# Two heads' low-part score passes on 64 rows each, side by side, in an fp32r attention stage

## Chip, cores and metric

The kernel runs on one core of a Trainium2 chip. The metric is the device time of one execution in microseconds; the kernel before is given as the median of three runs. Engines are named as the profile names them: PE (TensorE, with its weight loads as PEld), DVE (VectorE), ACT (ScalarE), POOL (GpSimd), SP (SyncE, which issues most transfers).

## What is computed

Two transformer blocks follow each other; the change touches the attention of the first. It has two kinds of heads over 1024 tokens and 256 context tokens, with a head size of 64:

```python
s_loc = einsum(q_block, k_window) * scale      # "a": 8 query heads on 2 key heads, a band of 128
s_ctx = einsum(q_block, k_ctx) * scale         # both kinds also see the context
p = softmax(concat([s_loc + mask, s_ctx, sink]))
o = p_loc @ v_window + p_ctx @ v_ctx
...
s_loc = einsum(q_block, k_rows) * scale + rpb  # "b": 8 heads, a neighbourhood in a 16 x 64 grid
```

The rest of the program (projections, two gated feed-forwards, a gated linear attention) is left as it is.

## The kernel before

fp32 products are made of fp32r passes: an operand is split into a high and a low part, and the products of the parts are summed in PSUM.

The attention is a list of 64 units x: 32 of kind "a" (8 token blocks, 4 pairs of heads), then 32 of kind "b" (4 pairs of heads, 8 token blocks). A unit is 128 queries of two heads, e = 0 and 1. An inner block has three key tiles of 128 and two of context, 640 score columns; the first and last token block have two key tiles, 512 columns. Units 0 to 3, 28 to 32, 39, 40, 47, 48, 55, 56 and 63 are the narrow ones.

Keys of a head stand stacked on 128 rows: `stack_k` (line 867) turns key tiles with PE and writes the high part to one half of the rows and the low part to the other. Queries stand doubled on both halves, once with their high parts and once with their low parts (`conv_q`, line 888, for two units at a time). So one pass over the 128 rows with the high query gives high x high and high x low, and a second one with the low query gives low x high and low x low.

A unit goes through these steps, each a function:

- `f_s(x, e)`, lines 936 to 950: the scores of one head, two passes (high, then low query), each over the local and the context columns in their own PSUM bank. A score tile takes two banks, and there are two of them (`ps_s`, bufs=2), which the heads use in turn.
- `f_max(x, e)`, line 961: DVE adds mask or bias and takes the row's extreme, in one operation that reads the scores; it frees the score tile.
- `f_exp(x, e)`, line 971: ACT.
- `f_pt(x, g)`, lines 981 to 998: PE turns up to four tiles of 128 x 128 of the probabilities into a tile `pp` (bufs=3). For g = 0 ACT copies it out (line 993) and POOL makes the high and low part (994, 995); for g = 1 and 2 ACT makes the high part from PSUM (997) and DVE the low part (998).
- `f_pv` (1011, 1016): probabilities times values; `f_fin` (1035, 1036): joins the halves.

The order is written out by hand in the loop over n at line 1179: unit n's scores and maxima stand beside unit n-1's exponentials, unit n-2's transposes, unit n-3's value products and unit n-4's end. `extra` hangs further steps on given n, the loading (`b_load`, 1072), turning and splitting of the "b" keys, values and biases among them. Each engine works through its own instructions in the order in which the program names them; SP's queue likewise.

Of the kernel before, what the change touches and what calls it, by code (L numbers as in the profile page):

```python
# [9 lines left out]
F32 = mybir.dt.float32  # L10
R32 = mybir.dt.float32r
# [7 lines left out]
P = 128  # L19
# [193 lines left out]
def kernel(ctx: ExitStack, tc: tile.TileContext, a: dict, out: bass.AP, dbg=None):  # L213
    nc = tc.nc
    ctx.enter_context(tc.manual_schedule())

    def pool(name, side=None, space=None, stack=None, bufs=1):
        kw = {}
        if side is not None:
            kw["side"] = side  # L220
        if space is not None:
            kw["space"] = space
        if space is not DRAM:
            kw["reuse_waits"] = "tile"
        return (stack or ctx).enter_context(tc.tile_pool(name=name, bufs=bufs, **kw))
# [14 lines left out]
    def tr(o, i, idn):  # L240
        nc.tensor.transpose(o, i, idn)
# [129 lines left out]
    KA = kva.tile([P, 10, 128], F32, name="KA")  # L371
# [109 lines left out]
    for j in range(4):  # L481
        c = slice(j * 512, j * 512 + 512)
# [299 lines left out]
    qraw, qhl = {}, {}  # L782
# [9 lines left out]
    def load_q(x):  # L792
        if x >= 32:
            return
        r = qp.tile([P, 4, 2, 64], F32, tag="qraw", name="qraw", bufs=3)
        for sl_, src in q_src(x):
            for e in range(2):
                nc.sync.dma_start(out=r[:, sl_, e, :], in_=src.rearrange("p (h d) -> p h d", d=64))
        qraw[x] = r
# [45 lines left out]
    ps_s = pool("ps_s", space=PSUM, stack=st_ps)  # L845
# [4 lines left out]
    b0 = pool("attn_b0", "left", stack=st_wk)  # L850
# [6 lines left out]
    st_a = ExitStack()  # L857
    aw = pool("attn_a", "right", stack=st_a)
    kstA = [aw.tile([P, 1280], R32, tag=f"kst{i}", name=f"kstA{i}") for i in range(2)]
    BP = [b0, None]  # L860
    B = {}
    A = {}

    def pp_tile():
        return ps_p.tile([P, 512], F32, tag="pp", name="pp", bufs=3)
# [15 lines left out]
    def kt(i):  # L881
        return [j for j in (i - 1, i, i + 1) if 0 <= j < 8]
# [5 lines left out]
    def conv_q(x):  # L888
        if x >= NU // 2:
            return  # L890
        r = qraw.pop(x)
        hl = [wk.tile([P, 4, P], R32, tag=f"q{e}", name=f"q{e}", bufs=2) for e in range(2)]
        pt = pp_tile()
        for j in range(4):
            tr(pt[:, j * P:(j + 1) * P], r[:, j].rearrange("p e d -> p (e d)"), ident)
        pv = pt.rearrange("p (h t) -> p h t", h=4)
        nc.scalar.activation(out=hl[0], in_=pv, func=AF.Copy)
        nc.vector.tensor_tensor(out=hl[1], in0=pv, in1=hl[0].bitcast(F32), op=ALU.subtract)
        qhl[x] = hl
        load_q(x + 3)  # L900

    def k_stack(u, e):
        return kstA[u[2] // 2] if u[0] == "a" else B["k", u[2]][e]
# [4 lines left out]
    def order(u, e):  # L908

        kk = kt(u[1])  # L910
        first = u[1] == 7 if u[0] == "a" else 0 < u[1] < 7 and e == 1
        return [8, 9] + kk if first else kk + [8, 9]
# [20 lines left out]

    st = {}

    def f_s(x, e):
        u = units[x]
        kk = kt(u[1])
        nl = len(kk) * P
        c1 = order(u, e)[0] == 8  # L940
        w = nl + 256
        a0 = 512 - (256 if c1 else nl)
        ps = ps_s.tile([P, 1024], F32, tag="s", name="ps_s", bufs=2)[:, a0:a0 + w]
        lo, co = (256, 0) if c1 else (0, nl)
        k = k_stack(u, e)
        for z in range(2):
            q = qhl[x // 2][z][:, 2 * (x % 2) + e]
            nc.tensor.matmul(ps[:, lo:lo + nl], q, k[:, kk[0] * P:kk[0] * P + nl], start=(z == 0), stop=(z == 1))
            nc.tensor.matmul(ps[:, co:co + 256], q, k[:, 1024:1280], start=(z == 0), stop=(z == 1))
        st["s", x, e] = ps  # L950

    def f_max(x, e):

# [12 lines left out]
    def f_exp(x, e):  # L966
        u = units[x]
        nm, sm = st["nm", x]
        sp = st["sp", x]
        w = len(kt(u[1])) * P + 256  # L970
        nc.scalar.activation(out=sp[:, e, :w], in_=sp[:, e, :w], func=AF.Exp, bias=nm[:, e:e + 1], scale=-1.0,
                             accum_out=sm[:, e:e + 1])

    def f_pt(x, gi):
        u = units[x]
        nk = len(kt(u[1])) + 2
        if gi == 0:
            st["pt", x] = wk.tile([P, 10, 2, P], R32, tag="pt", name="pt", bufs=2)
        pt = st["pt", x]
        sp = st["sp", x] if gi < 2 else st.pop(("sp", x))  # L980
        g = list(range(4 * gi, min(4 * gi + 4, 2 * nk)))
        if not g:
            return
        pp = pp_tile()
        for x_, b in enumerate(g):
            j, e = b // 2, b % 2
            tr(pp[:, x_ * P:(x_ + 1) * P], sp[:, e, j * P:(j + 1) * P], ident)
        w = len(g) * P
        ph, pl = pt[:, g[0]:g[0] + len(g), 0, :], pt[:, g[0]:g[0] + len(g), 1, :]
        pv = pp[:, :w].rearrange("p (b t) -> p b t", t=P)  # L990
        if gi == 0:
            pf = wk.tile([P, 4, P], F32, tag="pf", name="pf", bufs=2)
            nc.scalar.activation(out=pf, in_=pv, func=AF.Copy)
            nc.gpsimd.tensor_copy(out=ph, in_=pf)
            nc.gpsimd.tensor_tensor(out=pl, in0=pf, in1=ph.bitcast(F32), op=ALU.subtract)
        else:
            nc.scalar.activation(out=ph, in_=pv, func=AF.Copy)
            nc.vector.tensor_tensor(out=pl, in0=pv, in1=ph.bitcast(F32), op=ALU.subtract)
# [72 lines left out]

    def b_load(p):
        for n, d in (("kr", dkb), ("vr", dvb)):
            r = b0.tile([P, 10, 128], F32, tag=n, name=n)
            nc.sync.dma_start(out=r, in_=d[:, :, p * 128:p * 128 + 128].rearrange("t p c -> p t c"))
            B[n, p] = r

    def b_v(p, g):
        if g == 0:
            B["v", p] = BP[p % 2].tile([P, 10, 2, 128], R32, tag="vB", name="vB")  # L1080
        vr_ = B["vr", p][:, 2 * g:2 * g + 2].rearrange("p t (h d) -> p (t h) d", h=2)
# [4 lines left out]
    def b_k(p, g):  # L1086
        if g == 0:
            B["k", p] = [BP[p % 2].tile([P, 1280], R32, tag=f"kst{i}", name=f"kstB{i}") for i in range(2)]
        g0 = (8, 0, 4)[g]
# [10 lines left out]
    def b_bias(p, e):  # L1100
        if e == 0:
            B["bI", p] = BP[p % 2].tile([P, 1024], F32, tag="bI", name="bI")
            nc.gpsimd.memset(B["bI", p][:, 384:640], 0.0)
            B["bE", p] = BP[p % 2].tile([P, 2, 3, 16, 8], F32, tag="bE", name="bE")
        pb = pp_tile()
# [14 lines left out]
    def at(n, f, *args):  # L1120
        extra.setdefault(n, []).append((f, args))

    def switch_pools():
        st_a.close()
        st_kva.close()
        BP[1] = pool("attn_b1", "right", stack=st_b1)

    st_b1 = ExitStack()

    for p, load, ks, vs, bs in (  # L1130
        (0, 16, (18, 20, 22), (19, 21, 23, 25, 27), (24, 26)), (1, 33, (35, 36, 37), (36, 37, 38, 39, 40), (38, 39)),
        (2, 40, (42, 43, 44), (42, 43, 44, 45, 46), (45, 46)), (3, 48, (50, 51, 52), (50, 51, 52, 53, 54), (53, 54))):
        at(load, b_load, p)
        at(load, b_bload, p, 0)
        for g, n in enumerate(ks):
            at(n, b_k, p, g)
        for g, n in enumerate(vs):
            at(n, b_v, p, g)
        for g, n in enumerate(bs):
            at(n, b_bias, p, g)  # L1140
# [30 lines left out]
    for g0 in (8, 0, 4):  # L1171
        stack_k([KA[:, t] for t in range(g0, min(g0 + 4, 10))], kstA[0], kstA[1], g0 * P)
        if g0 == 0:
            conv_q(0)

    def ok(x):
        return 0 <= x < NU

    for n in range(NU + 5):
        if n == 35:  # L1180
            switch_pools()
        if ok(n):
            f_s(n, 0)
            f_max(n, 0)
        if ok(n - 1):
            f_exp(n - 1, 0)
        if ok(n - 2):
            f_pt(n - 2, 0)
        if ok(n):
            f_s(n, 1)  # L1190
            f_max(n, 1)
        if ok(n - 1):
            f_exp(n - 1, 1)
        if ok(n - 2):
            f_pt(n - 2, 1)
        if ok(n - 3):
            f_pv(n - 3, 0)
        if ok(n - 2):
            f_pt(n - 2, 2)
        if ok(n - 3):  # L1200
            f_pv(n - 3, 1)
        if ok(n - 4):
            f_fin(n - 4)
        if n % 2 == 0:
            conv_q(n // 2 + 1)
        for f, args in extra.get(n, []):
            f(*args)
# [246 lines left out]
    for n4 in range(2):  # L1454
# [8 lines left out]
        for t in range(8):  # L1463
            ps = early.pop(t, None)
            if ps is None:
                ps = ps_a.tile([P, 512], F32, tag="acc", name="pwo", bufs=4)
# [778 lines left out]
```

## Time and profile before

| what | value |
|---|---|
| median of three runs | 2665.67 us (2665.38 to 2666.24) |
| profiled execution | 2668.49 us, span 2666.7 us |
| mean granted PE clock | 0.991 |
| PE busy | 2576.5 us, 97% |
| DVE, ACT, POOL busy | 1645.7, 1058.8, 1148.6 us |
| first score pass to the start of the last unit | 312.7 to 609.2 us |

A busy time counts any recorded instruction of the engine; passes on PE overlap, and the record of one is longer than the distance to the next. Distances of starts tell more of PE's pace than busy times do.

### The profile page before, as it was taken

How to read it: one execution, taken by the hardware profiler on the slowest of the kernel's cores; microseconds unless marked ns; L12 is line 12 of the kernel's file. 1: busy time of each engine (PE TensorE's matmuls, PEld its weight loads, DVE VectorE, ACT ScalarE, POOL GpSimd, SP SyncE). 2: the span in 40 equal slices, each digit the busy share in tenths (PEclk: the TensorE clock that was granted, in tenths of full speed). 3: DMA queues.
4: the chain of work that ended last, by engine and by line, in shares of the span. 5: the costliest groups of instructions: out<-in, count | busy, mean ns of one | idle time of the engine just before them, and what ended most of it. 6: DMA issues, size and time to landing. Idle time of an engine off the chain costs nothing. (4 is left out here: it accounts for less than half of the span.)

```text
span 2666.7 us, 37138 instructions
## 1 busy us (share of the span) xinstructions
PE 2576.5 (97%) x14053; PEld 2154.0 (81%) x14053; DVE 1645.7 (62%) x3003; ACT 1058.8 (40%) x2613; POOL 1148.6 (43%) x1071
## 2 busy tenths in 40 slices
PE   7999999999989999999999999999999999999998
PEld 3999898899977888888878877877777777777786
DVE  3688678774565555555556432422777777777776
ACT  4644488785232222222223534322433333333333
POOL 2355355564446666666653221212333333333321
PEclk9999999999999999999999999999999999999999
DMA  6166522212111111111111111110111111111112
GB/s 245 33 192 200 147 56 54 73 49 88 33 40 48 48 52 59 48 48 55 56 48 41 50 48 32 32 48 32 49 39 48 48 48 48 48 48 48 48 48 87
DMA packets 152540, 170.87 MB, mean 64 GB/s; under 512 B 39444, under 2 KB 135460, under 8 KB 151336
## 3 DMA queue, kind: packets, MB, share of 16 engines
q1 hardware_dynamic: 152200, 168.35, 19.9%
q8 instruction: 111, 1.82, 0.3%
q0 software_dynamic: 160, 0.14, 0.1%
q14 instruction: 69, 0.57, 0.1%
HBM read 154.81 MB, written 13.65 MB: 63 GB/s over the span
## 5 line engine op out<-in xcount | busy, mean ns | idle before, releaser
L140 POOL TENSOR_TENSOR wlo<-raw,whi 128x512 fp32r<-128x512 f32 x132 | 176.7, 1343 | 476.7 <-ACT whi L139 447.8
L1697 PE MATMUL pgu<-h,whi 128*128 128x512 f32 x864 | 342.4, 396 | 3.1 <-DVE h L1633 3.1
L1698 PE MATMUL pgu<-h,wlo 128*128 128x512 f32 x864 | 341.2, 395 | 0.5 <-POOL wlo L140 0.5
L1696 PE MATMUL pgu<-h,whi 128*128 128x512 f32 x864 | 341.4, 395 | 0.0
L140 DVE TENSOR_TENSOR wlo<-raw,whi 128x512 fp32r<-128x512 f32 (+2 forms) x304 | 221.3, 741 | 149.5 <-ACT whi L139 148.9
L139 ACT ACTIVATE whi<-raw 128x512 fp32r<-128x512 f32 (+1 forms) x436 | 232.2, 552 | 151.1 <-DMA raw<-in_w_down 61.0
L1715 DVE TENSOR_TENSOR uv<-pgu,uv 128x512 f32<-128x512 f32 x216 | 147.7, 687 | 150.0 <-PE pgu L1698 128.6
L237 PE MATMUL pdn<-wlo,hid 128*128 128x512 f32 x576 | 227.3, 395 | 4.5 <-DVE wlo L140 4.5
L236 PE MATMUL pdn<-whi,hid 128*128 128x512 f32 x576 | 226.4, 393 | 1.3 <-DVE uv L1410 1.0
L238 PE MATMUL pdn<-whi,hid 128*128 128x512 f32 x576 | 226.6, 393 | 0.0
L1411 POOL TENSOR_TENSOR x<-x,uv 128x512 f32<-128x512 f32 x144 | 192.2, 1355 | 31.6 <-DVE uv L1410 28.7
L1697 PEld LDWEIGHTS pgu<-h,whi 128*128 128x128 f32 x864 | 162.3, 188 | 42.3 <-DVE h L1633 3.6
L1696 PEld LDWEIGHTS pgu<-h,whi 128*128 128x128 f32 x864 | 162.5, 188 | 40.1
L1698 PEld LDWEIGHTS pgu<-h,wlo 128*128 128x128 f32 x864 | 162.1, 188 | 39.9 <-POOL wlo L140 0.9
L1718 POOL TENSOR_TENSOR uv<-uv 128x512 f32<-128x512 f32 x72 | 109.7, 1524 | 169.1 <-DVE uv L1715 169.1
L1566 POOL TENSOR_TENSOR hid<-sg,hid 128x512 fp32r<-128x512 f32 x80 | 118.0, 1479 | 132.0 <-ACT hid L1565 129.9
L236 PE MATMUL pin<-whi,h 128*128 128x256 f32 x512 | 146.8, 287 | 6.1 <-ACT hsq L634 2.5
L237 PE MATMUL pin<-wlo,h 128*128 128x256 f32 x512 | 146.7, 286 | 1.7 <-DVE wlo L140 1.7
L238 PE MATMUL pin<-whi,h 128*128 128x256 f32 x512 | 146.5, 286 | 0.0
L237 PEld LDWEIGHTS pdn<-wlo,hid 128*128 128x128 f32 x576 | 108.1, 188 | 34.1 <-DVE wlo L140 9.6
L236 PEld LDWEIGHTS pdn<-whi,hid 128*128 128x128 f32 x576 | 108.2, 188 | 27.8 <-DVE uv L1410 1.5
L1407 DVE TENSOR_TENSOR x<-pdn,x 128x512 f32<-128x512 f32 x160 | 105.3, 685 | 38.8 <-PE pdn L238 29.0
(391 smaller groups left out, 6951.0 us busy)
## 6 DMA issues: line engine op xcount, KB each, us to landing
raw<-in_ffn_w_up SPq DMA_DIRECT2D x22, 1024.0 KB
mraw<-in_w_mod SPq DMA_DIRECT2D x32, 512.0 KB
raw<-in_w_gate SPq DMA_DIRECT2D x11, 1024.0 KB
raw<-in_w_up SPq DMA_DIRECT2D x11, 1024.0 KB
raw<-in_w_down SPq DMA_DIRECT2D x11, 1024.0 KB
raw<-in_ffn_w_down SPq DMA_DIRECT2D x11, 1024.0 KB
raw<-in_w_in SPq DMA_DIRECT2D x9, 1024.0 KB
wm<-in_w_mod SPq DMA_DIRECT2D x8, 1024.0 KB
```

What stands on the lines that cost most here:

```text
L139: nc.scalar.activation(out=hi, in_=src, func=AF.Copy)
L140: (engine or self.engine or nc.vector).tensor_tensor(out=lo, in0=src, in1=hi.bitcast(F32), op=ALU.subtract)
L236: nc.tensor.matmul(ps, lh, rh, start=(i == 0), stop=False)
L237: nc.tensor.matmul(ps, lh, rl, start=False, stop=False)
L238: nc.tensor.matmul(ps, ll, rh, start=False, stop=(i == n - 1))
L1411: nc.gpsimd.tensor_tensor(out=xs, in0=xs, in1=tmp, op=ALU.add)
L1566: nc.gpsimd.tensor_tensor(out=hl[:, c], in0=sg[:, cc, c], in1=hh[:, c].bitcast(F32), op=ALU.subtract)
L1696: nc.tensor.matmul(ps, lh, rh, start=start and k == 0, stop=False)
L1697: nc.tensor.matmul(ps, lh, rl, start=False, stop=False)
L1698: nc.tensor.matmul(ps, ll, rh, start=False, stop=stop and k == n - 1)
L1715: nc.vector.tensor_tensor(out=o, in0=ps, in1=u, op=ALU.add)
L1718: nc.gpsimd.tensor_tensor(out=o, in0=u, in1=v, op=ALU.add)
```

## The change

The two heads' scores of a unit are issued together, `f_s(x)`: first the high passes of both heads on 128 rows as before, then the low passes on 64 rows only, head 0 on rows 0 to 63, head 1 on rows 64 to 127, a pair of passes (one of each head) for the local columns and a pair for the context. The low query then meets the high keys alone; the product of the two low parts is left out. A "b" head has its high keys on the right rows already. For "a", where both heads of a unit share one key head, `kxA` holds the high keys on the other half of the rows, copied by two transfers from POOL's queue. Units 0 and 1 keep full low passes. In the loop the second part of the transposes moves ahead of the second head's maximum. The loads of the "b" keys move to other memory, and pair 1's keys, values and first bias rows are loaded at n = 35 instead of 33, with its key turning at 36 to 38 instead of 35 to 37.

```diff
+    kxA = aw.tile([P, 1280], R32, name="kxA")
...
-    def f_s(x, e):
+    def f_s(x):
...
-        k = k_stack(u, e)
-        for z in range(2):
-            q = qhl[x // 2][z][:, 2 * (x % 2) + e]
-            nc.tensor.matmul(ps[:, lo:lo + nl], q, k[:, kk[0] * P:kk[0] * P + nl], start=(z == 0), stop=(z == 1))
-            nc.tensor.matmul(ps[:, co:co + 256], q, k[:, 1024:1280], start=(z == 0), stop=(z == 1))
-        st["s", x, e] = ps
+        heads = []
+        for e in range(2):
+            c1 = order(u, e)[0] == 8
+            a0 = 512 - (256 if c1 else nl)
+            ps = ps_s.tile([P, 1024], F32, tag="s", name="ps_s", bufs=2)[:, a0:a0 + nl + 256]
+            lo, co = (256, 0) if c1 else (0, nl)
+            heads.append([(ps[:, lo:lo + nl], slice(kk[0] * P, kk[0] * P + nl)),
+                          (ps[:, co:co + 256], slice(1024, 1280))])
+            st["s", x, e] = ps
+        q = [[qhl[x // 2][z][:, 2 * (x % 2) + e] for z in range(2)] for e in range(2)]
+        for e in range(2):
+            for o_, c in heads[e]:
+                nc.tensor.matmul(o_, q[e][0], k_stack(u, e)[:, c], start=True, stop=False)
+        if x < 2:
...
+            return
+        for i in range(2):
+            for e in range(2):
+                o_, c = heads[e][i]
+                r = slice(64 * e, 64 * e + 64)
+                k = kxA if u[0] == "a" and u[2] // 2 != e else k_stack(u, e)
+                nc.tensor.matmul(o_, q[e][1][r], k[r, c], start=False, stop=True)
...
-            r = b0.tile([P, 10, 128], F32, tag=n, name=n)
+            r = KA if n == "kr" and p == 0 else (BP[1] if n == "kr" else b0).tile([P, 10, 128], F32, tag=n, name=n)
...
-        (0, 16, (18, 20, 22), (19, 21, 23, 25, 27), (24, 26)), (1, 33, (35, 36, 37), (36, 37, 38, 39, 40), (38, 39)),
+        (0, 16, (18, 20, 22), (19, 21, 23, 25, 27), (24, 26)), (1, 35, (36, 37, 38), (36, 37, 38, 39, 40), (38, 39)),
...
+    for e in range(2):
+        nc.gpsimd.dma_start(out=kxA[64 - 64 * e:128 - 64 * e], in_=kstA[e][64 * e:64 * e + 64])
...
-            f_s(n, 0)
+            f_s(n)
             f_max(n, 0)
         if ok(n - 1):
             f_exp(n - 1, 0)
         if ok(n - 2):
             f_pt(n - 2, 0)
+        if ok(n - 2):
+            f_pt(n - 2, 1)
         if ok(n):
-            f_s(n, 1)
             f_max(n, 1)
         if ok(n - 1):
             f_exp(n - 1, 1)
-        if ok(n - 2):
-            f_pt(n - 2, 1)
```

How PE's instructions stand. In the kernel before, one inner "a" unit (ps_s: scores; pp from sp: the transposes; po: value products; the numbers behind q tell the high query, 5499, from the low one, 5500):

```order
L948 MATMUL ps_s<-kstA_3996,q_5499 128x384
L949 MATMUL ps_s<-kstA_3996,q_5499 128x256
L948 MATMUL ps_s<-kstA_3996,q_5500 128x384
L949 MATMUL ps_s<-kstA_3996,q_5500 128x256
L241 MATMUL pp<-ident,sp 128x128 x4
L948 MATMUL ps_s<-kstA_3996,q_5499 128x384
L949 MATMUL ps_s<-kstA_3996,q_5499 128x256
L948 MATMUL ps_s<-kstA_3996,q_5500 128x384
L949 MATMUL ps_s<-kstA_3996,q_5500 128x256
L241 MATMUL pp<-ident,sp 128x128 x4
L1011 MATMUL po<-pt,VA 128x256 x6
```

The same unit in the change (high query 5501, low query 5502):

```order
L956 MATMUL ps_s<-kstA_3996,q_5501 128x384
L956 MATMUL ps_s<-kstA_3996,q_5501 128x256
L956 MATMUL ps_s<-kstA_3996,q_5501 128x384
L956 MATMUL ps_s<-kstA_3996,q_5501 128x256
L967 MATMUL ps_s<-kxA,q_5502 128x384
L967 MATMUL ps_s<-kstA_3996,q_5502 128x384
L967 MATMUL ps_s<-kxA,q_5502 128x256
L967 MATMUL ps_s<-kstA_3996,q_5502 128x256
L241 MATMUL pp<-ident,sp 128x128 x8
L1028 MATMUL po<-pt,VA 128x256 x6
```

The four transposes that stood between the heads' scores now stand behind both heads, eight in a row.

DVE, two inner "a" units of the kernel before (ISA: the maximum and the reading of its result; pt: the low part of the transposes, four tiles, then two):

```order
L961 ISA sp,stat<-ps_s,maskA,nsink 128x640
L961 ISA stat 128x1
L961 ISA sp,stat<-ps_s,maskA,nsink 128x640
L961 ISA stat 128x1
L998 TENSOR_TENSOR pt<-pp,pt 128x4x128
L998 TENSOR_TENSOR pt<-pp,pt 128x2x128
L1036 COPY o_3966<-pp 128x128
```

And of the change:

```order
L978 ISA sp,stat<-ps_s,maskA,nsink 128x640
L978 ISA stat 128x1
L1015 TENSOR_TENSOR pt<-pp,pt 128x4x128
L978 ISA sp,stat<-ps_s,maskA,nsink 128x640
L978 ISA stat 128x1
L1015 TENSOR_TENSOR pt<-pp,pt 128x2x128
L1053 COPY o_3966<-pp 128x128
```

The second head's maximum has moved behind the subtraction for the second transposes.

## Rows read from the trace of the kernel before

**Rows 1.** The page, part 1: busy us, share of the span, instructions.

```profile
PE 2576.5 (97%) x14053; PEld 2154.0 (81%) x14053; DVE 1645.7 (62%) x3003; ACT 1058.8 (40%) x2613; POOL 1148.6 (43%) x1071
```

**Rows 2.** Table by stretches: us, busy time and count by engine, clock, DMA.

```profile
360.00:400.00 40.00, 39.08 (x313) 37.74 (x312) 31.07 (x76) 35.60 (x88) 21.41 (x24) 1.00 0.27 67
```

**Rows 3.** Waits from 335 to 440 us: total us, times, longest.

```profile
PEld pp L241 <- DVE pt L998: 8.1, 15, 1.3
```

**Rows 4.** Timeline, PE, unit 17: start us, length, line, operation.

```profile
383.27 0.42 PE L948 MATMUL ps_s<-kstA,q 128*128 128x384 f32 x1
...
383.65 0.34 PE L948 MATMUL ps_s<-kstA,q 128*128 128x384 f32 x1
383.83 0.28 PE L949 MATMUL ps_s<-kstA,q 128*128 128x256 f32 x1
383.95 0.60 PE L241 MATMUL pp<-ident,sp 128*128 128x128 f32 x4
...
387.19 0.42 PE L948 MATMUL ps_s<-kstA,q 128*128 128x384 f32 x1
```

**Rows 5.** Timeline, PE, a later stage: passes on 64 rows among others on 128.

```profile
1826.63 0.40 PE L1939 MATMUL pr<-h,whi 128*128 128x512 f32 x1
1826.87 0.39 PE L1940 MATMUL pr<-h,wlo 128*128 128x512 f32 x1
1827.19 0.30 PEld L2063 LDWEIGHTS pu<-v,kdG 64*128 64x128 f32 x4 [0.36 <-issue]
...
1827.51 0.38 PE L2063 MATMUL pu<-v,kdG 64*128 64x256 f32 x2
...
1827.82 0.50 PE L1938 MATMUL pr<-h,whi 128*128 128x512 f32 x1
```

**Rows 6.** Timeline, all engines, units 16 and 17: transposes, copies, subtractions.

```profile
377.68 0.86 ACT L997 ACTIVATE pt<-pp 128x512 fp32r<-128x512 f32 x2
378.37 1.02 DVE L998 TENSOR_TENSOR pt<-pp,pt 128x512 fp32r<-128x512 f32 x2 [0.36 <-ACT pt L997]
...
379.39 0.60 PE L241 MATMUL pp<-ident,sp 128*128 128x128 f32 x4
...
380.11 0.60 ACT L993 ACTIVATE pf<-pp 128x512 f32<-128x512 f32 x1 [0.30 <-PE pp L241]
...
382.11 1.02 DVE L998 TENSOR_TENSOR pt<-pp,pt 128x512 fp32r<-128x512 f32 x2 [0.59 <-ACT pt L997]
382.52 0.38 ACT L1022 ACTIVATE oT<-po 128x256 f32<-128x256 f32 x1
382.71 0.41 DVE L998 TENSOR_TENSOR pt<-pp,pt 128x256 fp32r<-128x256 f32 x1
382.85 0.66 PE L241 MATMUL pp<-ident,qraw 128*128 128x128 f32 x4
```

**Rows 7.** Groups by shape, DVE, 312 to 615 us: busy, mean ns, idle.

```profile
L961 DVE CUSTOM_DVE_ANT_0 sp<-ps_s,maskA,nsink 128x640 f32<-128x640 f32 x48 | 40.4, 875 | 0.5
L961 DVE CUSTOM_DVE_ANT_0 sp<-ps_s,maskA,nsink 128x512 f32<-128x512 f32 x16 | 11.5, 747 | 4.0 <-POOL maskA L1168 2.7 <-PE ps_s L949 1.2
```

**Rows 8.** Timeline, PE: the first pass of units 2, 6, 16, 31, 35.

```profile
322.20 0.55 PE L948 MATMUL ps_s<-kstA,q 128*128 128x256 f32 x1
...
335.52 0.42 PE L948 MATMUL ps_s<-kstA,q 128*128 128x384 f32 x1
...
378.72 0.42 PE L948 MATMUL ps_s<-kstA,q 128*128 128x384 f32 x1
...
451.14 0.37 PE L948 MATMUL ps_s<-kstA,q 128*128 128x256 f32 x1
...
465.21 0.42 PE L948 MATMUL ps_s<-kstB,q 128*128 128x384 f32 x1
```

**Rows 9.** Timeline, POOL: the first split after the masks.

```profile
324.95 0.61 POOL L994 CAST pt<-pf 128x512 fp32r<-128x512 f32 x1 [5.76 <-ACT pf L993]
```

More of the change, by code (lines that the diff above doesn't have):

```diff
@@ L939, in f_s @@
         nl = len(kk) * P
[L940 to L944, printed above, removed]
-        k = k_stack(u, e)
-        for z in range(2):
-            q = qhl[x // 2][z][:, 2 * (x % 2) + e]
-            nc.tensor.matmul(ps[:, lo:lo + nl], q, k[:, kk[0] * P:kk[0] * P + nl], start=(z == 0), stop=(z == 1))
-            nc.tensor.matmul(ps[:, co:co + 256], q, k[:, 1024:1280], start=(z == 0), stop=(z == 1))
-        st["s", x, e] = ps
+        heads = []
[13 more added lines that the diff above has]
+            for e in range(2):
+                for o_, c in heads[e]:
+                    nc.tensor.matmul(o_, q[e][1], k_stack(u, e)[:, c], start=False, stop=True)
+            return
[5 more added lines that the diff above has]
+                nc.tensor.matmul(o_, q[e][1][r], k[r, c], start=False, stop=True)
     def f_max(x, e):
@@ L1174 @@
             conv_q(0)
+    for e in range(2):
+        nc.gpsimd.dma_start(out=kxA[64 - 64 * e:128 - 64 * e], in_=kstA[e][64 * e:64 * e + 64])
     def ok(x):
```

## Prediction

> **What bounds the kernel now.** I read the page first: PE is busy 97% of the span, DVE 62%, ACT 40% [rows 1]. A share over the span says nothing about one stage, so the table by stretches comes next. In a stretch of the attention loop PE is busy 39.1 of 40 us, DVE 31.1, ACT 35.6 [rows 2]. Then the waits: in 105 us of the loop the largest of PE's own, transposes whose weight loads wait for DVE's subtraction (line 998), sums to 8.1 us [rows 3]. So PE's own work nearly sets the pace, and DVE and ACT have slack. I number the units 0 to 63; unit 17 is shown pass by pass [rows 4]: it takes 3.92 us, and nothing stands idle in its score passes.
>
> **Price of the low passes before.** A pass over 384 columns is followed by the next after 0.18 us, one over 256 after 0.12; no weight load shows between them [rows 4]. A head's low passes cost 0.30, a unit's two heads 0.60 us. Where a unit has 512 columns (256 and 256) it is 4 x 0.12 = 0.48. The first two units keep their passes. That leaves 48 units of 640 columns and 14 of 512.
>
> **Price of the low passes after.** The trace has passes on 64 rows side by side, in a later stage: line 2063 [rows 5]. Two share one record of 0.38 us at 1827.51: they start and end together, so pairing works there. But the change of row mode is not free. The 512-column pass before them started at 1826.87, and one of its kind is followed after 0.23 or 0.24 (1826.63 to 1826.87), so the next was due at 1827.10; the first 64-row load begins at 1827.19, 0.09 later. That load lies bare, as does the one of the first 128-row pass behind (0.50 recorded against 0.39, so 0.11). From 1827.19 to the second pair at 1827.51 it is 0.32; less the load, 0.21 are columns. On leaving, the last pair starts at 1827.51, streams 0.21, and the 128-row pass is recorded from 1827.82: 0.10 later, with its load bare. A transposition's load is shorter: 0.06, from 0.66 against 0.60 for four [rows 6]. So the new section costs 0.09 + 0.11 + 0.18 + 0.12 + 0.10 + 0.06 = 0.66 us against 0.60, and 0.60 against 0.48 on 512 columns. Halving the streaming by 0.30 is paid back by two changes of mode. As PE's work alone: 48 x 0.06 + 14 x 0.12 = **+4.6 us**. The Trainium skill (TensorE: Matmul & The Clock Gate, Part 3: Packing small matmuls) gives a packed group the span of one matmul plus about 4 ns per further tile; by it 0.60 would become about 0.30, some 18 us less over the 62 units. The rows carry the pairing and refuse the rest of it.
>
> **Price of the order.** The two score buffers are one per head. Before, the second head's scores of the next unit came after its first transposes, long after this unit's second maximum. Now they come 0.30 us into the next unit, and DVE's second maximum has moved behind the subtraction of the second transposes, which wants ACT's copy, which wants PE's transposes, which stand behind both heads' scores. That is a loop around one unit. From the second head's first score pass: its high passes 0.30; the low section up to its last column 0.50; leaving and load 0.16; four transposes up to their result 0.60 [rows 4, 6]; ACT's start 0.12 later (379.99 to 380.11); its first copy holds ACT 0.48 (0.86 for two, of 512 and 256 columns, less 0.38 for the short one), the second takes 0.60; DVE starts 0.10 after it (377.68 and 0.60, to 378.37, rounded up) and is held 0.60 (382.11 to 382.71); the maximum takes 0.88; for PE's start I put 0.06, between nothing and the 0.12 above [rows 6, 7]. Sum **4.40 us**. With 512 columns, 0.06 less twice and a maximum of 0.75: 4.15 [rows 7]. I use the same two lengths in the second half of the units.
>
> A unit now lasts the longer of PE's work and this loop. It closes where units were shorter [rows 8]:
> - Units 2 to 5 took 13.32 us in all; 2 x 4.15 + 2 x 4.40 = 17.10: +3.8.
> - The odd units 7 to 19, seven of 3.89 to 3.92 like unit 17: 7 x 0.49 = +3.4. Their even neighbours, like unit 16 with 4.55 (378.72 to 383.27), can't give it back, for the loop holds each unit alone.
> - Units 31 to 34 took 14.07; again 17.10: +3.0.
> - The other 47 (37 wide, 10 narrow) I let pay for the passes alone: 37 x 0.06 + 10 x 0.12 = +3.4.
>
> Sum **+13.6 us**. A loop 0.2 shorter, its steps overlapping more than I have it, takes 15 x 0.2 off: +10.6; one 0.2 longer gives +16.6.
>
> **The small edits.** Two issues for kxA go to POOL's queue, which idles 5.76 us up to 324.95 [rows 9]; the first user is unit 2, after 322.20. I take 0, and up to +2 if the copy lands late. The key and value loads of pair 1 start two units later, one unit ahead of their transposes instead of two. A unit of over 4 us is left to them; I take 0, and up to +5, one whole unit, if other transfers hold them. The first pair's key rows in KA: KA is dead once stacked, so 0. The transposes' move costs PE nothing in itself; the pp buffers they want are freed by DVE, whose wait [rows 3] may shrink a little. I take 0 there too.
>
> The profiled execution was 2668.5 us (span 2666.7), 2.8 above the median of the runs, 2665.7. Added to its own time the sum gives 2682.1; against the median, **2679.3**.
>
> **The rivals.**
> - *The row mode is free* (the other side). If the fp32r passes' loads slip under the pass before, as 128-row loads do, the section costs 0.30 and the loop falls by 0.36 to 4.04 (3.79 with 512 columns). The same count: +2.3 in units 2 to 5, +0.9 in the seven, +1.6 in 31 to 34, and 37 x 0.30 + 10 x 0.24 = 13.5 off in the others, -8.7: 2657.0. It decides from the point where the first 64-row load starts with the last high pass instead of 0.09 after it. For it: the second pair's load does lie under the first pair. Against it: every entry and exit of line 2063 that I read shows the gap. Chance 0.10. This is the case in which the Trainium skill's span rule, cited above, would hold.
> - *The loop does not close*: DVE gets through the second maximum before PE asks. Only the passes' price stays: +4.6, 2670.3. For it: DVE is idle for a fifth of the loop's stretches [rows 2]. Against it: an idle DVE is also what a loop looks like when each of its engines waits in turn. Chance 0.15.
> - *The change doesn't pair*: line 2063's pairs start a buffer; these accumulate in one, at twice the column rate. If their writes can't go on together, each section is 0.30 longer (narrow 0.24), the loop 4.70 (4.39): +4.9, +5.5, +4.1 and 47 x 0.36 = 16.9, together +31.4: 2697.1. Chance 0.12.
> - Forecast as above, 0.63.
>
> **How the numbers follow.** The runs can tell about 0.2%, 5.3 us, from nothing. The likeliest case alone, its loop from 0.2 short to 0.2 long and the transfers late, covers 2676 to 2689. The range takes in the second rival, the near edges of the first and third, 2662 to 2694. Faster by 0.2%: most of the first rival, 0.08. Within it: the second rival, the rest of the first and a low tail of the forecast, 0.20. Slower: 0.72.
>
> **What would show it.** Right: between the last high pass and the first low load 0.09 idle, each section about 0.66, the two heads' low passes starting within 0.01; PE's score passes newly waiting for the second maximum (DVE stat or bstat), in the odd units 7 to 19 and in units 2 to 5 and 31 to 34, which last about 4.4 and 4.15. Wrong: no such wait, or loads that begin with the pass before.

## The result, and the profile after

The changed kernel takes 2684.31 us (median of six runs, 2681.08 to 2686.73), the kernel before in the same job 2666.1: 1.0061 times as long, interval 1.0051 to 1.0071. The profiled execution took 2683.55 us, span 2681.8, against 2668.49 and 2666.7: 15.1 us more by either, where 13.6 was forecast. By the two medians it is 18.2 us more, by the ratio 16.3. One of e6's eight executions took 5082.02 us, nearly twice the others, and stands outside its ratio.

The page of the changed kernel, part 1, and its table by stretches (us from:to, length, busy us and count of each engine, granted clock, DMA share, GB/s), answer to [rows 1, 2]. In what follows line 956 is the high passes, 967 the low ones, 978 the maximum, 1010 and 1014 ACT's copies, 1015 DVE's subtraction, 241 the transposes, 1123 (1106 in e5) a bias pass into the same buffers.

```profile
PE 2586.3 (96%) x14053; PEld 2135.5 (80%) x14053; DVE 1644.4 (61%) x3003; ACT 1057.4 (39%) x2613; POOL 1148.5 (43%) x1073
```

```profile
360.00:400.00 40.00, 38.16 (x300) 32.97 (x299) 29.63 (x75) 32.25 (x82) 18.89 (x20) 1.00 0.24 60
```

Every engine does less in the same 40 us (PE 300 instructions against 313), and none has come nearer to full. So no engine became the bound; they wait for each other. The waits of 335 to 450 us, PE's own, show for what. First the kernel before, then the changed one (us in total, times, longest):

```profile
PE pp L241 <- DVE pt L998: 6.2, 12, 1.1
```

```profile
PE ps_s L956 <- DVE stat L978: 6.2, 13, 1.1
PE pp L241 <- DVE pt L1015: 1.6, 4, 0.5
PE pp L1123 <- DVE pt L1015: 1.0, 2, 0.5
```

The wait for a transposes' buffer has shrunk to 1.6 and 1.0 us, and PE's score passes wait for DVE's maximum instead, as the forecast had it. The timeline of the changed kernel shows one turn (start us, length, engine, line, operation; in brackets the idle time before and what ended it):

```profile
379.84 0.56 PE L956 MATMUL ps_s<-kstA,q 128*128 128x384 f32 x2 [0.42 <-DVE stat L978]
...
380.33 0.44 PE L967 MATMUL ps_s<-kxA,q 64*128 64x384 f32 x1
...
380.33 0.44 PE L967 MATMUL ps_s<-kstA,q 64*128 64x384 f32 x1
...
380.62 0.28 PE L967 MATMUL ps_s<-kxA,q 64*128 64x256 f32 x1
...
380.83 1.09 PE L241 MATMUL pp<-ident,sp 128*128 128x128 f32 x8
...
381.58 0.60 ACT L1010 ACTIVATE pf<-pp 128x512 f32<-128x512 f32 x1 [1.21 <-PE pp L241]
...
382.07 0.59 ACT L1014 ACTIVATE pt<-pp 128x512 fp32r<-128x512 f32 x1
...
382.77 0.69 DVE L1015 TENSOR_TENSOR pt<-pp,pt 128x512 fp32r<-128x512 f32 x1 [0.95 <-ACT pt L1014]
...
383.38 0.88 DVE L978 CUSTOM_DVE_ANT_0 sp<-ps_s,maskA,nsink 128x640 f32<-128x640 f32 x1
...
384.31 0.56 PE L956 MATMUL ps_s<-kstA,q 128*128 128x384 f32 x2
...
384.59 0.28 PE L956 MATMUL ps_s<-kstA,q 128*128 128x256 f32 x1
...
384.80 0.18 PEld L967 LDWEIGHTS ps_s<-kxA,q 64*128 64x128 f32 x1 [0.19 <-issue]
...
384.91 0.19 PEld L967 LDWEIGHTS ps_s<-kxA,q 64*128 64x128 f32 x1
...
385.08 0.27 PE L967 MATMUL ps_s<-kxA,q 64*128 64x256 f32 x1
...
385.29 0.86 PEld L241 LDWEIGHTS pp<-ident,sp 128*128 128x128 f32 x8 [0.19 <-issue]
...
388.80 0.56 PE L956 MATMUL ps_s<-kstA,q 128*128 128x384 f32 x2 [0.29 <-DVE stat L978]
```

The loop reads from top to bottom: second head's high passes, low pairs, eight transposes, ACT's two copies, the subtraction, the second maximum. The second heads of the next two units start at 384.31 and 388.80: turns of 4.47 and 4.49 us, or 4.48 a unit, where I had added up 4.40. The pairs do start together: 380.33 twice.

Where the 15.1 us came in, from the first score pass of each unit to that of a later one (us). The last two columns are two of the experiments below:

| units | before | after | more | forecast | e1 | e3 |
|---|---|---|---|---|---|---|
| 0, 1 | 9.47 | 9.95 | +0.5 | 0 | 9.79 | 9.81 |
| 2 to 5 | 13.31 | 19.39 | +6.1 | +3.8 | 15.34 | 15.22 |
| 6 to 30 | 115.63 | 120.86 | +5.2 | +4.7 | 110.76 | 109.63 |
| 31 to 34 | 14.07 | 17.28 | +3.2 | +3.0 | 14.63 | 14.41 |
| 35 to 62 | 143.99 | 143.97 | 0.0 | +2.0 | 142.81 | 140.09 |
| all 63 | 296.47 | 311.45 | +15.0 | +13.5 | 293.33 | 289.15 |

### The profile page after: what moved, and what is told of

Its sections match the earlier page's. It is cut to its first block, busy times and chain, and to the rows that moved or that the text cites. A ratio compares the mean times of both kernels' runs of the same rounds, so it can differ in the third digit from the quotient of the medians.

```text
span 2681.8 us, 37159 instructions
## 1 busy us (share of the span) xinstructions
PE 2586.3 (96%) x14053; PEld 2135.5 (80%) x14053; DVE 1644.4 (61%) x3003; ACT 1057.4 (39%) x2613; POOL 1148.5 (43%) x1073
```

## Experiments

My theory is that the order makes a loop that PE waits on, and that the row mode costs a little besides. The rival: the 64-row passes with their mode changes cost it all. Two edits, alone and together, tell them apart.

**e1: the loop taken away, the 64-row pairs kept.**

```diff
         if ok(n - 2):
             f_pt(n - 2, 0)
-        if ok(n - 2):
-            f_pt(n - 2, 1)
         if ok(n):
             f_max(n, 1)
+        if ok(n - 2):
+            f_pt(n - 2, 1)
```

> The changed kernel with one thing put back: the second head's maximum stands ahead of the subtraction for the second transposes again. Scores together and passes on 64 rows stay. Loop theory (the second head's scores wait for that maximum, which waits for the transposes behind both heads' scores): the loop opens, PE no longer waits for the second maximum, and only the price of the row mode is left, 0.06 us in 48 units and 0.12 in 14, +4.6 us against before: ratio 1.0017, between 0.999 and 1.003. Row-mode theory (the passes on 64 rows cost all of the loss on PE): nothing changes, 1.006.

Measured: 2663.57 us, 0.9988 times the kernel before (0.9979 to 0.9996). Its waits in 335 to 450 us:

```profile
PE pp L241 <- DVE pt L1015: 2.5, 3, 1.3
```

No wait for a maximum is left, and the loss is gone with it, the pairs still there. By the forecast's terms, pairs alone at +4.6, it should even have come out above the kernel before; e6 tells why it didn't.

**e2: the order of the change, low passes on 128 rows** (so low x low is computed again), and **e3: e1 and e2 together**.

```diff
-        if x < 2:
+        if x < NU:
```

> The changed kernel with all low passes on 128 rows as in the first two units (the copies into kxA stay, unread); the order of scores, transposes and maxima stays. Loop theory: the loop is only 0.06 us shorter (0.60 of streaming for a section of 0.66), so most of the loss stays: +9 to +12 us against before, ratio 1.003 to 1.005. Row-mode theory: the loss is gone, 1.000.

> Both put back: low passes on 128 rows, the second maximum ahead of the subtraction; the heads' scores stay together. Both theories: no loss, 0.998 to 1.001. What tells: the distance to the kernel with the maximum first alone is the price of the row mode where no loop is in the way, 4.6 us by the loop theory's sum, some 16 by the row-mode theory.

Measured: e2 2679.9 us, 1.0045 times (1.0031 to 1.0059); e3 2661.64, 0.998 times (0.9971 to 0.9989). The waits of e2, with no pass on 64 rows in it:

```profile
PE ps_s L956 <- DVE stat L978: 5.9, 13, 1.1
PE pp L241 <- DVE pt L1015: 1.6, 4, 0.5
PE pp L1123 <- DVE pt L1015: 1.0, 2, 0.5
```

These are the changed kernel's waits almost to the tenth. By the medians the order costs 18.3 us with full rows (e2 less e3) and 20.7 with pairs (after less e1); the row mode costs 1.9 us without the loop (e1 less e3) and 4.4 with it (after less e2). The intervals overlap in both of the last two, and one profiled execution of each kernel gives other sizes over the 63 units: 4.2 us without the loop (293.33 less 289.15) and 2.8 with it (311.45 less 308.62 for e2). So the row mode costs some 2 to 4 us, where 4.6 was forecast, and the runs don't settle it more closely. Either way it is small beside the loop, and the rival falls.

**e4: twice as many changes of row mode.** The local columns' high passes of both heads are followed by their low pair, then the context's by theirs, so each unit enters and leaves the 64-row mode twice.

```diff
-        for e in range(2):
-            for o_, c in heads[e]:
-                nc.tensor.matmul(o_, q[e][0], k_stack(u, e)[:, c], start=True, stop=False)
...
         for i in range(2):
+            for e in range(2):
+                o_, c = heads[e][i]
+                nc.tensor.matmul(o_, q[e][0], k_stack(u, e)[:, c], start=True, stop=False)
             for e in range(2):
                 o_, c = heads[e][i]
                 r = slice(64 * e, 64 * e + 64)
```

> The changed kernel with the mode changes doubled: local high passes of both heads, local low pair, then context high passes, context low pair. The columns are the same. A second entry and exit add 0.09 + 0.11 + 0.10 + 0.11 = 0.41 us to a unit, on the loop and on PE alike: 62 x 0.41 = +25 us against the changed kernel, ratio to before about 1.0155. If the pairs' price lay elsewhere (in the columns, in PSUM), nothing is added: 1.006.

Measured: 2707.42 us, 1.0151 times (1.0137 to 1.0165), 23.1 more than the change. The price of a change of mode stands; here it lies inside the loop too, so each unit pays it. Not all of the 23 us is the mode, though. The new order also puts the first head's context pass behind the second head's first pass, which is inside the loop. The two lines show e4's second head and its transposes:

```profile
386.21 0.44 PE L963 MATMUL ps_s<-kstA,q 128*128 128x384 f32 x1 [0.32 <-DVE stat L979]
...
387.70 0.33 PE L241 MATMUL pp<-ident,sp 128*128 128x128 f32 x1
```

From one to the other it is 1.49 us, against 0.98 in the changed kernel (384.31 to 385.29). Of the 0.51 more, 0.12 are that context pass.

**e5: the other half of the change alone.** The kernel before, each head with its own passes, and the second transposes ahead of the second head's scores:

```diff
         if ok(n - 2):
             f_pt(n - 2, 0)
+        if ok(n - 2):
+            f_pt(n - 2, 1)
         if ok(n):
             f_s(n, 1)
             f_max(n, 1)
         if ok(n - 1):
             f_exp(n - 1, 1)
-        if ok(n - 2):
-            f_pt(n - 2, 1)
```

> The kernel before with one half of the change alone: each head keeps its own score passes, all on 128 rows, and the second transposes' parts stand ahead of the second head's scores and its maximum, as in the change. Loop theory: the order costs only because scores of both heads stand ahead of the transposes on PE; here the second head's scores stand behind them, and the maximum of the unit before, on which they wait, is done by then. So no waits for a maximum on PE in 335:440 (after: 6.0 and 7.0 us over the span), the waits for the transposes' buffers fall from 6.2 us to about 2.5 as without the loop (e1, e3), and the time is 2655 to 2664 us. Rival, the early parts cost by themselves (ACT's copy and DVE's subtraction ahead of a maximum that PE needs): the waits for a maximum stay and the time is about 2680 us.

Measured: 2658.99 us, 0.9969 times (0.9956 to 0.9981): faster than both kernels, the fastest median of the study. Its waits in 335 to 450 us:

```profile
PE pp L241 <- DVE pt L998: 3.0, 9, 0.5
PE pp L1106 <- DVE pt L998: 0.5, 1, 0.5
```

No wait for a maximum, and PE's buffer waits fall from 6.2 to 3.5 us. So the early transposes are no cost by themselves. They hurt only with both heads' scores ahead of them and the second maximum behind their subtraction; e1 has the first without the second, and no loss. Whether the gain is theirs, e6 tells.

**e6: what held the kernel before.** Its order with only the second exponential moved behind ACT's copy of the second transposes:

```diff
         if ok(n):
             f_s(n, 1)
             f_max(n, 1)
-        if ok(n - 1):
-            f_exp(n - 1, 1)
         if ok(n - 2):
             f_pt(n - 2, 1)
+        if ok(n - 1):
+            f_exp(n - 1, 1)
```

> The kernel before, with the second head's scores and maximum where they were, but its exponential behind ACT's copy of the second transposes instead of ahead of it. If what bounds the kernel before in its loop is PE's wait for a transposes' buffer (6.2 us in 335:450), held by a subtraction on DVE that waits for that copy, which waits for an exponential of about 0.7 us, the waits fall to under 3 us and the time is 2658 to 2664 us. Rival, the buffer is held by DVE's own queue (the second maximum ahead of the subtraction): waits and time within 2 us of before.

Measured: 2660.85 us, 0.9974 times (0.9964 to 0.9985). Its waits there:

```profile
PE pp L241 <- DVE pt L998: 2.9, 5, 1.0
```

More than half of the 6.2 us of waits before came from ACT's order: a transposes' buffer stayed full while ACT did an exponential first, and DVE's queue, the rival, was left as it was. In e1, e3 and e5 the second exponential stands behind that copy too, and all four beat the kernel before. The changed kernel has it so as well, but there the loop takes more than it gives. In the profiled executions e6 needs 288.43 us for the 63 units and e5 288.94, so the exponential's place alone gives about all that e5 gained; nothing shows a gain of the early transposes beyond it.

**e7: the clock in units 2 to 5.** These cost 6.1 us where 3.8 was forecast. The changed kernel (first row), the kernel before (second) and e7 (third), 326 to 330 us; the clock is the third number from the end:

```profile
326.00:330.00 4.00, 3.11 (x15) 2.62 (x13) 1.96 (x4) 3.08 (x7) 1.89 (x2) 0.50 0.24 55
```

```profile
326.00:330.00 4.00, 4.00 (x35) 4.00 (x34) 3.65 (x9) 4.00 (x12) 2.84 (x3) 1.00 0.29 66
```

```profile
326.00:330.00 4.00, 3.10 (x19) 2.66 (x19) 2.00 (x5) 3.08 (x7) 1.89 (x2) 0.82 0.26 59
```

PE comes to unit 2 at a granted clock of 0.50, 1.2 GHz; in 318 to 322 us, just before, it was busy 1.87 of 4 us after the change and 1.96 before it. The kernel before is back at 1.00 by 326 us, the changed one still at 0.50. e7 gives PE more to do in the units' waits, work whose result is overwritten:

```diff
+        if 2 <= x < 6:
+            for o_, c in heads[0]:
+                nc.tensor.matmul(o_, q[0][0], k_stack(u, 0)[:, c], start=True, stop=True)
         for e in range(2):
             for o_, c in heads[e]:
```

> The changed kernel, with the first head's high-part passes of units 2 to 5 made twice (the first result is overwritten): 8 matmuls of 0.3 to 0.4 us more, each pair standing where PE waits 0.5 to 0.9 us for the second maximum. If the low granted clock (0.50 up to 330 us) is what makes units 2 to 5 cost 6.1 us instead of the 3.8 forecast, and lasts because PE waits there, PE is busy over 0.95 of 326:330 (after: 3.11 of 4 us), the clock rises before 330 us, and units 2 to 5 take 17 to 18.5 us instead of 19.4. Rival, the loop alone sets these units whatever the clock: 19.4 us or up to 1.5 us more, at the same clock.

Measured: 2683.95 us, 1.0058 times (1.0046 to 1.0071), no different from the change in its runs. In the profiled execution the clock is 0.82 in 326 to 330 and units 2 to 5 take 18.23 us instead of 19.39, within what was expected, but PE is busy 3.10 us there, not the 3.8 I wanted, for part of its work, added passes included, ran at the higher clock and took less time. So some 1.2 of the missing 2.3 us went with the clock, in one execution of each kernel; that my passes raised it is not shown, since in e8, which has none of them, it is 0.87 in the same stretch.

**e8: one term of the loop longer by 0.69.** The changed kernel with DVE's subtraction of the second transposes made twice.

```diff
-            nc.vector.tensor_tensor(out=pl, in0=pv, in1=ph.bitcast(F32), op=ALU.subtract)
+            for _ in range(2 if gi == 1 else 1):
+                nc.vector.tensor_tensor(out=pl, in0=pv, in1=ph.bitcast(F32), op=ALU.subtract)
```

> The changed kernel, with the subtraction of the second transposes' low parts on DVE made twice in every unit: 0.69 us more of DVE per unit, ahead of the second maximum. Loop theory: the subtraction is a term of the loop, so units 6 to 30 go from 120.9 us to about 138 (25 x 0.69 = 17.3 more), units 31 to 34 take some 2.8 more, units 35 to 62 at most a few us more since they wait for a maximum in 3.2 us only; in all 2702 to 2712 us. Rival, the loop does not hold and PE is the bound (DVE is busy about 0.7 of these stretches): under 3 us more, up to 2687 us.

Measured: 2726.14 us, 1.022 times (1.0206 to 1.0234). Its largest waits in 335 to 450 and, in the second fence, 501 to 664 us, its units 35 to 62:

```profile
PE ps_s L956 <- DVE stat L978: 12.8, 11, 1.8
```

```profile
PE ps_s L956 <- DVE bstat L978: 10.1, 11, 1.5
```

Units 6 to 30 take 139.1 us, 18.2 more (17.3 expected), units 31 to 34 2.9 more (2.8). With DVE busy only 29.6 of 40 us in the changed kernel, an operation made twice is paid in full: that is a loop. But units 35 to 62 took 18.6 more, where I expected a few at most. The loop lay close under PE's own work there; the few waits of the changed kernel (3.2 us for a maximum in 480 to 624 us) did not mean slack.

## Why the prediction was right

**What bounds and what takes over: right.** The loop exists, in units 2 to 34, with the wait that was named; e1 takes it away, e2 keeps it without any 64-row pass, e8 stretches it. Its sum of 4.40 us measured 4.48. One step was short: the first pass after a wait shows its weight load bare, so the second head's second pass follows after 0.28 us (384.31 to 384.59), where 0.18 was put. The other steps came within 0.02 of what was put.

**How it acts: not quite as put.** I let it hold "each unit alone", the odd ones at 4.40. From second head to second head it does, but counted from first pass to first pass, odd units such as unit 9 went from 3.91 to 4.04 only, and the even ones carry the rest (unit 8: 4.55 to 4.93). The wait stands in front of the second head, and what it pushes falls into the unit that starts next. For units 8 and 9 together it is 8.97 against 8.46, +0.51, and I had +0.49 and +0.06. Only the place within the pair was wrong.

**Units 2 to 5: mis-sized**, +6.1 for +3.8. The term took the loop's length from stretches at full clock. In 322 to 338 us the granted clock was 0.93 before, and 0.69 in the changed kernel one microsecond later, as its units are:

```profile
322.00:338.00 16.00, 15.91 (x124) 15.82 (x124) 12.85 (x34) 13.89 (x34) 8.02 (x9) 0.93 0.15 34
```

```profile
323.00:339.00 16.00, 14.14 (x78) 12.00 (x78) 7.78 (x18) 9.16 (x22) 5.62 (x6) 0.69 0.10 23
```

In e7 about half of the missing 2.3 us went with the clock. The table tells more: e3, with neither the loop nor a 64-row pass, also takes 1.9 us more than the kernel before in these units, at a clock of 0.80 in 322 to 338 us. From e1, which loses 2.0, to the changed kernel it is 4.05 us, and that share, the loop's (at a clock lower still), is near the 3.8 put. So most of what was missing is not the loop's. The clock is its likely cause; that is not shown.

**The price of the low passes: right in its steps.** The last high pass starts at 384.59 and a pass of its length is followed after 0.12 us; the first 64-row load begins at 384.80, the 0.09 later that was put. From the first 64-row load to the second pair it is 0.28 us (384.80 to 385.08; 0.29 put), from there to the transposes 0.21 (0.22 put). PEld idles 0.19 us ahead of the first 64-row load and again ahead of the transposes' first, so neither load lies under the pass before it. For the columns of a pair the sum took 0.18 and 0.12 us, the pace of the 128-row passes, although the reading above it had 0.21 for a pair of 256 columns; it gave no reason, and the 0.28 and 0.21 bear it out. The whole, put at 4.6, came to 1.9 us by the medians of e1 and e3 and 4.2 by their profiles, and e4 paid 23 us for a second change of mode and a longer loop. Of the rule of the Trainium skill cited above (TensorE: Matmul & The Clock Gate, Part 3: Packing small matmuls) one half agrees: the heads' passes start within 0.01 us and end together. The other does not hold here, since its span counts no entry and exit: the section saves 0.30 us of columns and pays 0.09, 0.11, 0.10 and 0.06, about as much, for going in and out.

**The transposes' buffers: the term that was put at nothing.** I took their shorter waits as 0, without working them out. They went from 6.2 to 2.6 us in 335 to 450 us, and the table shows the worth: in e1 units 6 to 30 take 110.8 us, less than the 115.6 before, pairs and all, and e6, which only shortens these waits, gained 7.3 us. It also answers for units 35 to 62: there e1 takes 2.7 us more than e3 (2.0 put for the passes), yet the change took no more than before. Against what this order could give, the loop costs 18 to 21 us, not the 9 that I counted against the kernel before. The total came out near the sum because the gain left out stood against a loop taken too small; that part is luck.

The transfers for kxA, and pair 1's later loads, cost nothing that shows. Ahead of unit 2's first 64-row load PEld idles 0.2 us and the trace names the copy of kxA, but unit 3, with no copy to wait for, idles as long at the same place (0.23 us at 324.27 and at 329.83). Units 35 to 62 lost no time. The rivals of a free row mode, of a loop that does not close, and of passes that do not pair are each refused by a row above.

## What to carry to other kernels

When two steps are put together on an in-order engine, write down the loop that the new order makes through all engines, from a buffer's release back to it, and add up its terms; an engine busy for three quarters of a stretch does not mean slack, and doubling one term on the chip tells at once. Cost the good half of a change by itself: here the early transposes, with the exponential behind them, gave 0.9969 of the time before, the exponential's place alone 0.9974, and a maximum moved behind a subtraction turned that into a loss once the scores were paired. Narrow passes side by side halve the columns, but must be long enough, or many enough in a row, to pay for going in and out of the mode.

## What was not expected of the hardware

The clock's recovery was different between programs with much the same work in hand: 326 to 330 us had 1.00 before, 0.50 after, 0.82 in e7 and 0.87 in e8. These are single executions, so program and chance can't be told apart. It can also fall again. Two stretches of e8 in which PE was busy little over half the time are followed by one at 0.59, though PE is busy throughout it:

```profile
326.00:330.00 4.00, 2.38 (x19) 1.85 (x19) 3.14 (x7) 2.09 (x7) 0.88 (x1) 0.87 0.29 66
330.00:334.00 4.00, 2.26 (x17) 1.65 (x16) 2.32 (x6) 2.26 (x7) 1.89 (x2) 0.99 0.00 0
334.00:338.00 4.00, 4.00 (x24) 4.00 (x24) 1.89 (x4) 2.28 (x5) 1.89 (x2) 0.59 0.02 6
```

So a new wait may cost a second time, through the clock of the work behind it; no run here takes the two apart.
